# One hybrid layer (attention, S5, mixture of experts): another order for the work between the attention scores and the output projection

## The chip, the cores and the metric

The kernel runs on one core of a Trainium2 chip. The metric is the device time of one execution in microseconds (us), lower is better. Engines are named as in the profile: PE is TensorE, DVE is VectorE, ACT is ScalarE, POOL is GpSimd, SP is SyncE, whose queue issues nearly all loads here.

## What is computed

One layer on 272 token rows (16 learned meta tokens and 256 frames) of width 1024. The attention and an S5 state-space model run beside each other on projections of the same rows; their outputs are put side by side and multiplied with `w_out`. Then come a residual, a layer norm, and a mixture of 32 experts, four per token.

```python
h = layer_norm(concat(meta_tokens, x), ln_in_g, ln_in_b)
proj = h @ w_in                                  # q, k, v, u
# 4 heads, each the difference of two softmaxes
p = softmax(q @ k.T + bias)                      # masked by chunks of 64 frames
w = p[0] - lam * p[1]
att = rms_norm(w @ v, subln_g) * (1 - lam_init)
# S5: 32 groups of 16 channels, 64 states each
y = C @ scan(Abar, Bbar @ u) + d_skip * u
y = gelu(y); ssm = y * sigmoid(y @ w_glu + b_glu)
mix = concat(att, ssm) @ w_out
h = layer_norm(2 ** 0.25 * h + mix, ln1_g, ln1_b)
# router: top 4 of 32 experts, softmax over the four
ffn = sum over the four of gate * (((up + 1) * g * sigmoid(1.702 * g)) @ w_down + b_down)
out = layer_norm(2 ** 0.25 * h + ffn, ln2_g, ln2_b)[16:]
```

## The kernel before

The kernel is one function. It is written out by hand: each engine has one queue and works through it in the order in which the program issues its instructions, waiting at each for the semaphores of what it needs. An instruction that waits holds everything behind it on its engine. So the order of the calls in the program is the order of the work on every engine.

**The stages.** First the input rows are normalized (`hr`, kept for the residual) and projected to u, q, k and v. Beside the projections VectorE, GpSimd and ScalarE build the S5 matrices. Four frames make one step of the scan; inside such a step the output depends on the input through *lag blocks*, small matrices for lags 0 to 3. Then come the attention scores and the part that this change is about, the mix, the norm, the router, and a sorting of the tokens by expert. The longest stage is the last: the weights of the 32 experts, 384 chunks of 1 MiB, stream through a ring of 19 buffers (half-tiles) while TensorE multiplies. `load_to(n)` issues the chunk loads up to number n from SyncE, in order; a load waits until its buffer is free, and holds the loads behind it.

**From the scores to the mix**, in program order:

- *Lag blocks.* Matmuls write the products of all lags into one PSUM bank (`kb_`). VectorE builds the lag diagonal from a copied identity (`m32`) and the skip weights (`Dm`), eight pieces. `lag_b` (L719) copies the bank to SBUF (`KS`, ScalarE), adds the diagonal (VectorE), and copies 16 pieces into the padded lag matrix `ML`, eight on each of the two engines (L728, L730).
- *Value projections.* `values(h)` (L641) projects the values of head h and copies them out of PSUM (`vT`, L643). `value_rows(h, vT)` (L646) transposes them and copies them to `vr` with ScalarE (L650, L651). Heads 0 and 1 are done before; `values(2)`, `lag_b`, `values(3)` follow, then the load of the attention half of `w_out` (`wo0`), the router and bias loads, and `split_w(1, ...)`.
- *Rounding.* `split_w(j, ...)` (L568) prepares four 128-row tiles of `w_out`, j = 1 the S5 half and j = 0 the attention half. ScalarE rounds each (128 x 1024) to a high part (L572), VectorE subtracts it for the low part (L574). The mix adds three products: high by high, low weight by high row, high weight by low row (`cl`).
- *Attention products.* `av_a(i)` (L758 and on) does block i of 128 query rows: per head it transposes the weights, copies them to `wT` (ScalarE the full 128-row parts, L767; VectorE the 16-row part, L768), and multiplies with `vr` (L783), one head behind the transposes. Block 0 sees 144 keys, block 1 sees 272. In block 0 each head is followed by two pieces of `residual_rows` (L500): VectorE multiplies a 128 x 512 piece of `hr` by the norm's gain or adds its bias (L505), eight pieces in all. `av_b(i)` squares and sums the result (ScalarE, L791), takes the power -1/2 (GpSimd, L195) and scales (VectorE, L793). `av_c(i)` transposes it back (L800) and writes high and low parts (VectorE, L802 and L803).
- *S5 outputs.* `out_a(fb)` adds a lag product (L813) and two state products (L815) for four groups of 128 columns, evicted by ScalarE (`yt`, L818). `out_b` transposes two of them (L826) and does the GELU, ending in a tanh (L833); `out_c` writes `gy`.
- *Mix.* `mix(i, kbs)` (L863) accumulates the three products for tiles kbs of `w_out` and rows of block i, in four PSUM banks. The four attention tiles come first. Between them `split_bias` splits the experts' biases into three bf16 pieces (VectorE and ScalarE, L875 to L884). Then the gate: four matmul groups with `w_glu`, a sigmoid (ScalarE), a multiplication (VectorE, L900), and high and low parts (L901, L902). The S5 tiles of the mix follow (from 158.50 us on).

PSUM banks are given out in rotation by `nb()`: who takes a bank waits for the last reader of the one that had it eight banks before. The calls around the change stand in this order: `av_a(0)`, `av_b(0)`, half a rounding of `wo0`, `out_a(0)`, `out_a(1)`, `av_a(1)` with the other half inside, `av_c(0)`, `av_b(1)`, `out_b(0)`, `out_a(2)`, `out_a(3)`, `load_to(7)`, `out_c(0)`, `av_c(1)`, `out_b(1)`, then the mix.

Of the kernel before, what the change touches and what calls it, by code (L numbers as in the profile page):

```python
# [15 lines left out]
AF = mybir.ActivationFunctionType  # L16
OP = mybir.AluOpType
# [47 lines left out]
def hybrid_layer(ctx, tc, I, out):  # L65
    nc = tc.nc
    V, S, G, T, SP = nc.vector, nc.scalar, nc.gpsimd, nc.tensor, nc.sync
# [6 lines left out]
    PS = psp.tile([128, 8, 512], F32, name="PS")  # L74
# [9 lines left out]
    def slot(i, shape, name, dt=F32):  # L84
        return per.tile(shape, dt, name=name, tag=f"slot{i}")
# [414 lines left out]
    def residual_rows(n):  # L500

        for _ in range(n):
            i, h, j = rr_todo.pop(0)
            hf = hr[:, i, h * 512:(h + 1) * 512]
            V.tensor_tensor(hf, hf, bc[:, j, h * 512:(h + 1) * 512], op=(OP.mult, OP.add)[j])  # L505
# [54 lines left out]
    def load_to(n):  # L560
        while nload[0] < min(n, len(stream)):
            chunk(nload[0])
            nload[0] += 1
# [4 lines left out]
    def split_w(j, s_, l_, ks):  # L568
        if j not in W_HI:
            W_HI[j], W_LO[j] = parts4(s_, "wh", FR), parts4(l_, "wl", FR)  # L570
        for k in ks:
            S.activation(W_HI[j][k], W_OUT[j][k], AF.Copy)  # L572
        for k in ks:
            V.tensor_sub(W_LO[j][k], W_OUT[j][k], W_HI[j][k].bitcast(F32))  # L574
# [66 lines left out]
    def values(h):  # L641
        vT = lw([128, NP], "vT", bufs=2)
        S.activation(vT, proj("v", h, 0), AF.Copy)  # L643
        return vT

    def value_rows(h, vT):  # L646
        b = nb()
        for blk, n in ((0, 128), (1, 128), (2, 16)):
            T.transpose(PS[:n, b, blk * 128:blk * 128 + 128], vT[:, blk * 128:blk * 128 + n], ident)
        S.activation(vr[:, 0:2, h * 128:(h + 1) * 128], PS[:, b, 0:256].rearrange("p (a e) -> p a e", a=2), AF.Copy)  # L650
        S.activation(vr[:16, 2, h * 128:(h + 1) * 128], PS[:16, b, 256:384], AF.Copy)  # L651
# [45 lines left out]
    def lt_(shape, name, tag=None, bufs=None):  # L697
        return lpool.tile(shape, F32, name=name, tag=tag or name, bufs=bufs)

    kb_ = nb()  # L700
# [10 lines left out]
                         AB[:, ri, P, 0:3].rearrange("p t g c -> p (t g c)"), start=(ri == 0), stop=(ri == 1))  # L711
    Dm = lt_([128, 4, 32], "Dm", tag="y1")
    m32 = lt_([128, 32], "m32")
    for q in range(4):
        V.tensor_copy(m32[32 * q:32 * q + 32], ident[32 * q:32 * q + 32, 32 * q:32 * q + 32])
    for fb in range(4):
        V.tensor_scalar(Dm[:, fb], m32, DSK[:, fb:fb + 1], None, op0=OP.mult)

    def lag_b():  # L719
        KS = lt_([128, 4, 128], "KS", tag="y0")  # L720
        S.activation(KS, PS[:, kb_].rearrange("p (f c) -> p f c", f=4), AF.Copy)
        V.tensor_add(KS[:, :, 0:32], KS[:, :, 0:32], Dm)
        for j in range(4):
            for t in range(4):
                dst = ML[32 * t:32 * t + 32, :, j, 32 * t:128]
                srcv = KS[32 * j:32 * j + 32, :, 0:128 - 32 * t]
                if t < 2:
                    V.tensor_copy(dst, srcv)  # L728
                else:
                    S.activation(dst, srcv, AF.Copy)  # L730

    vt0 = values(2)
    lag_b()
    load_to(3)
    vt1 = values(3)
    wo0 = slot(3, [128, 4, D], "wo0")
    W_OUT[0] = [wo0[:, k] for k in range(4)]
    load(wo0, "w_out", 0, [[D, 128], [128 * D, 4], [1, D]])
# [5 lines left out]
    load(rk, "order_table", 0, [[2 * NE + 5, 128], [1, 2 * NE + 5]])  # L744
    for j, n in enumerate(("b_gate", "b_up", "b_down")):
        load(bf[32 * j:32 * j + 32], n, 0, [[D, 32], [1, D]])
    split_w(1, 5, 0, (0, 1, 2, 3))
    value_rows(2, vt0)
    value_rows(3, vt1)
    load_to(5)  # L750


    cat = mt([128, 8, NT], "cat", FR, tag="hTcat")
# [4 lines left out]
    def av_a(i, between=None):  # L758
        blks = ((0, 128), (1, 16)) if i == 0 else ((0, 128), (1, 128), (2, 16))
        nf = len(blks) - 1  # L760
        wts = []
        for h in range(4):
            tb = nb()
            for blk, n in blks:
                T.transpose(PS[:n, tb, blk * 128:blk * 128 + 128], PW[h, i][:, blk * 128:blk * 128 + n], ident)
            wT = lt_([128, 3, 128], "wT", bufs=2)
            S.activation(wT[:, :nf], PS[:, tb, :nf * 128].rearrange("p (a q) -> p a q", a=nf), AF.Copy)  # L767
            V.tensor_copy(wT[:16, nf], PS[:16, tb, nf * 128:nf * 128 + 128])  # L768
            wts.append(wT)
            if i == 0:  # L770
                residual_rows(2)
            if h == 1 and between:
                between()
            if h == 0:
                ob = nb()
            else:
                av_mm(i, h - 1, wts[h - 1], ob, blks, nf)
        av_mm(i, 3, wts[3], ob, blks, nf)
        OB[i] = ob
# [6 lines left out]
    def av_b(i):  # L786
        ob = OB[i]
        ss = lt_([128, 4], "ss")
        on = lt_([128, 4, 128], "on")
        for h in range(4):  # L790
            S.activation(on[:, h], PS[:, ob, h * 128:(h + 1) * 128], AF.Square, accum_out=ss[:, h:h + 1])  # L791
        rstd_of(ss, ss, EPS, 1.0 / 128)
        V.tensor_tensor(on, PS[:, ob].rearrange("p (h e) -> p h e", h=4), ss[:, :, None].to_broadcast([128, 4, 128]),  # L793
                        op=OP.mult)
        ON[i] = on

    def av_c(i):
        b = nb()
        for h in range(4):
            T.transpose(PS[:, b, h * 128:(h + 1) * 128], ON[i][:, h], ident)  # L800
        srcv, c_ = PS[:, b].rearrange("p (h e) -> p h e", h=4), slice(i * 128, (i + 1) * 128)
        V.tensor_scalar(cat[:, 0:4, c_], srcv, subg, None, op0=OP.mult)  # L802
        V.scalar_tensor_tensor(cl[0][:, :, c_], srcv, subg, cat[:, 0:4, c_].bitcast(F32), op0=OP.mult, op1=OP.subtract)  # L803
# [18 lines left out]
    def out_b(f2):  # L822
        b = nb()
        for f in range(2):
            for t in range(4):
                T.transpose(PS[:, b, f * 256 + t * 64:f * 256 + t * 64 + 64],  # L826
                            YT[2 * f2 + f][:, t * 128:(t + 1) * 128], ident[:64, :64])
        hy, ya = (lt_([128, 2, 4, 64], f"y{j}") for j in range(2))
        S.activation(hy, PS[:, b].rearrange("p (f t c) -> p f t c", f=2, t=4), AF.Copy)
        S.activation(ya, hy, AF.Square)  # L830
        V.tensor_scalar(ya, ya, 4 * 0.044715, 1.0, op0=OP.mult, op1=OP.add)
        V.tensor_mul(ya, ya, hy)
        S.activation(ya, ya, AF.Tanh, scale=2.0 * math.sqrt(2.0 / math.pi))  # L833
        HY[f2] = hy, ya
# [5 lines left out]
                                   op0=OP.add, op1=OP.mult)  # L840

    av_a(0)
    av_b(0)
    split_w(0, 8, 2, (0, 1))
    out_a(0)
    out_a(1)
    av_a(1, lambda: split_w(0, 8, 2, (2, 3)))
    av_c(0)
    av_b(1)
    out_b(0)  # L850
    out_a(2)
    out_a(3)
    load_to(7)
    out_c(0)
    av_c(1)
    out_b(1)


# [28 lines left out]
    out_c(1)  # L887
    split_bias()
    mix(1, range(2))
    mix(0, range(2, 4))  # L890
    mix(1, range(2, 4))
    gs = lw([128, 4, NT], "gs", tag="aw1")
# [658 lines left out]
```

## Time and profile before

| | |
|---|---|
| time, median of 3 runs | 1141.91 us (1139.74 to 1143.63) |
| the profiled execution | 1141.39 us, of which the profile's span is 1139.6 us |
| mean granted TensorE clock | 0.954 |
| TensorE matmul busy | 1021.1 us (90%) |
| VectorE busy | 365.6 us (32%) |
| ScalarE busy | 159.7 us (14%) |
| GpSimd busy | 106.5 us (9%) |
| loads of the main queue | 424.58 MB, 91.5% of the 16 DMA engines' time |

A busy share is an average over the whole span. Most of the span is the expert stage; the stretch of the change lies between about 100 and 172 us. The timelines of the engines in that stretch give, for each run of instructions of one line, its start, its length and their count, and in brackets how long the engine had been idle and what it had waited for. A float32 matmul appears as two records. The granted clock is the share of 2.4 GHz that TensorE was given.

### The profile page before, as it was taken

How to read it: one execution, taken by the hardware profiler on the slowest of the kernel's cores; microseconds unless marked ns; L12 is line 12 of the kernel's file. 1: busy time of each engine (PE TensorE's matmuls, PEld its weight loads, DVE VectorE, ACT ScalarE, POOL GpSimd, SP SyncE). 2: the span in 40 equal slices, each digit the busy share in tenths (PEclk: the TensorE clock that was granted, in tenths of full speed). 3: DMA queues.
4: the chain of work that ended last, by engine and by line, in shares of the span. 5: the costliest groups of instructions: out<-in, count | busy, mean ns of one | idle time of the engine just before them, and what ended most of it. 6: DMA issues, size and time to landing. Idle time of an engine off the chain costs nothing. (4 is left out here: it accounts for less than half of the span.)

```text
span 1139.6 us, 16409 instructions
## 1 busy us (share of the span) xinstructions
PE 1021.1 (90%) x6572; PEld 523.6 (46%) x6572; DVE 365.6 (32%) x755; ACT 159.7 (14%) x329; POOL 106.5 (9%) x223
## 2 busy tenths in 40 slices
PE   6986997899999788998999977799999999998665
PEld 5875884344554244444444423354453444453222
DVE  7999664223122212321131221122223212232103
ACT  1735423000010000111001000010001000001000
POOL 2300004101100110021001010101101010010001
PEclk9989898999999999998999987999999999999698
DMA  7725286999999999999999999999999999999795
GB/s 220 282 95 173 96 343 263 379 371 420 420 421 422 420 420 421 421 421 419 422 422 420 420 421 421 421 420 421 421 422 421 421 421 401 422 420 420 309 419 229
DMA packets 72313, 425.67 MB, mean 374 GB/s; under 512 B 14925, under 2 KB 15546, under 8 KB 23210
## 3 DMA queue, kind: packets, MB, share of 16 engines
q1 hardware_dynamic: 72234, 424.58, 91.5%
q8 instruction: 53, 0.87, 0.3%
q14 instruction: 26, 0.21, 0.1%
HBM read 423.50 MB, written 1.87 MB: 373 GB/s over the span
## 5 line engine op out<-in xcount | busy, mean ns | idle before, releaser
L1206 PE MATMUL PS<-wx,xgp 128*32 128x256 f32 (+2 forms) x3008 | 485.4, 493 | 30.6 <-DMA wx<-in_w_gate 20.9
L1206 PEld LDWEIGHTS PS<-wx,xgp 128*32 128x32 f32 (+2 forms) x3008 | 184.9, 133 | 292.9 <-issue 204.8
L1206 PE MATMUL PS<-wx,yT 128*32 128x256 f32 (+2 forms) x1504 | 230.3, 467 | 18.2 <-DMA wx<-in_w_down 16.2
L1206 PEld LDWEIGHTS PS<-wx,yT 128*32 128x32 f32 (+2 forms) x1504 | 90.7, 127 | 141.6 <-issue 89.8
L948 POOL COPY si<-P 96x32 bf16<-96x32 bf16 (+2 forms) x32 | 7.4, 233 | 755.4 <-PE PS L1200 725.5
L1253 DVE COPY yc<-PS 32x256 f32<-32x256 f32 (+1 forms) x39 | 20.0, 514 | 164.1 <-ACT yc L1255 164.1
L1159 PEld LDWEIGHTS PS<-ohp,hr 128*128 128x128 f32 x512 | 63.5, 200 | 8.4 <-issue 8.4
L1159 PE MATMUL PS<-ohp,hr 128*128 128x128 f32 x512 | 65.8, 288 | 0.2 <-DVE ohp L1151 0.2
L1228 DVE TENSOR_SCALAR PS<-PS 128x256 f32<-128x256 f32 (+2 forms) x33 | 22.6, 683 | 115.5 <-PE PS L1206 115.5
L1200 PE MATMUL PS<-B,si 96*32 96x256 bf16 (+2 forms) x282 | 40.2, 336 | 16.5 <-SPq L1309 9.6
L1222 DVE TENSOR_SCALAR g<-PS 128x256 f32<-128x256 f32 (+1 forms) x27 | 14.9, 553 | 120.5 <-PE PS L1206 120.4
L1239 DVE COPY yT<-PS 128x512 f32<-128x512 f32 (+1 forms) x39 | 22.7, 594 | 88.2 <-PE PS L1238 88.2
L1255 ACT ACTIVATE yc<-PS 32x256 f32<-32x256 f32 (+1 forms) x39 | 17.4, 446 | 231.2 <-PE PS L1206 224.9
L1290 DVE SCALAR_TENSOR_TENSOR lo<-yc,gc,hi 128x1024 fp32r<-128x1024 f32 x15 | 19.3, 1284 | 86.8 <-ACT hi L1289 85.5
L1304 DVE TENSOR_TENSOR acc<-PS,acc 128x1024 f32<-128x1024 f32 x30 | 35.4, 1220 | 14.7 <-PE PS L1301 14.6
L1163 ACT ACTIVATE xgp<-PS 128x512 f32<-128x512 f32 x16 | 9.6, 598 | 210.3 <-PE PS L1159 210.3
L1200 PEld LDWEIGHTS <-si 96*32 96x32 bf16 (+2 forms) x282 | 11.4, 101 | 49.2 <-issue 46.6
L1223 ACT ACTIVATE PS<-g 128x256 f32<-128x256 f32 (+1 forms) x27 | 13.2, 491 | 144.4 <-DVE g L1222 144.4
L1149 POOL TENSOR_SCALAR gop<-io,PMs,Gs 128x32 f32<-128x32 f32 (+2 forms) x60 | 33.2, 568 | 0.0
L1222 DVE TENSOR_SCALAR yc<-PS 128x1024 f32<-128x1024 f32 x6 | 7.3, 1225 | 78.5 <-PE PS L1206 78.5
L1301 PE MATMUL PS<-hi,gt 128*128 128x512 f32 x60 | 26.2, 437 | 3.0 <-ACTq L1309 3.0
L1247 ACT ACTIVATE yc<-PS 128x1024 f32<-128x1024 f32 x6 | 6.1, 1025 | 138.0 <-PE PS L1206 138.0
(389 smaller groups left out, 865.1 us busy)
## 6 DMA issues: line engine op xcount, KB each, us to landing
wx<-in_w_gate SPq DMA_DIRECT2D x128, 1024.0 KB, 19.7
wx<-in_w_up SPq DMA_DIRECT2D x128, 1024.0 KB, 19.8
wx<-in_w_down SPq DMA_DIRECT2D x127, 1024.0 KB, 19.7
w_u<-in_w_in SPq DMA_DIRECT2D x2, 1024.0 KB
w_q<-in_w_in SPq DMA_DIRECT2D x1, 2048.0 KB
w_k<-in_w_in SPq DMA_DIRECT2D x2, 1024.0 KB
w_v<-in_w_in SPq DMA_DIRECT2D x1, 2048.0 KB
wo<-in_w_out SPq DMA_DIRECT2D x2, 1024.0 KB
```

Source lines behind the costliest of these rows:

```text
L1149: eng.tensor_scalar(dst[:, i, o:o + m], iv, pc, gg[:, i, t:t + 1], op0=OP.is_equal, op1=OP.mult)
L1159: T.matmul(PS[:, 4 + h, k * 128:k * 128 + n], hr[:, i, rows_of(db)], oh_[:, i, :n], start=(i == 0), stop=(i == 1))
L1200: T.matmul(o, sel[:, :m], B96[:, w, f * n:f * n + n], start=True, stop=False)
L1206: T.matmul(PS[(f % nf) * m:(f % nf) * m + m, b + f // nf, :n], xT(kb), c[:, f * n:f * n + n], start=False, stop=(kb == 7))
L1222: V.tensor_scalar(g_, r_, 7.0, None, op0=OP.min)
L1228: V.tensor_scalar(r_, r_, 7.0, -7.0, op0=OP.min, op1=OP.max)
L1239: V.tensor_copy(yT[:, 4 * a:4 * a + nk], PS[:, b, :nk * 128].rearrange("p (k s) -> p k s", k=nk))
L1253: V.tensor_copy(d_, s_)
L1255: S.activation(d_, s_, AF.Copy)
L1290: V.scalar_tensor_tensor(lo[:n], YC[g][:n], GC[g][:n], hi[:n].bitcast(F32), op0=OP.mult, op1=OP.subtract)
L1301: T.matmul(PS[:, 4 + 2 * i + h], GT[g][:n, i * 128:(i + 1) * 128], part[:n, h * 512:(h + 1) * 512], start=(j == 0), stop=(j == 1))
L1304: V.tensor_tensor(acc[:, i].rearrange("p (h c) -> p h c", h=2), PS[:, 4 + 2 * i:6 + 2 * i], acc[:, i].rearrange("p (h c) -> p h c", h=2), ...
```

## The change

It puts the same work into another order, and moves eight small operations to another engine:

- The lag diagonal (`m32`, `Dm`) is built by GpSimd in place of VectorE.
- The lag products leave their PSUM bank right behind the value projection of head 2. The rest of `lag_b`, the add and the sixteen copies, comes behind the first attention product (`av_a(0)`).
- The value rows of heads 2 and 3 follow their projections at once, ahead of the load of `wo0`.
- The rounding of the S5 half of `w_out`, which stood ahead of the value rows, is cut in two, on both sides of the second attention product. The rounding of the attention half is cut in two as well: behind `av_b(1)`, and behind `av_c(1)`.
- The second attention product comes ahead of the first two S5 outputs, `av_b(1)` behind them.
- The chunk loads 2 and 3 (`load_to(3)`) and 4 and 5 (`load_to(5)`) are issued later.
- The eight residual pieces leave the first attention product and stand behind the first attention tiles of the mix.

```diff
-        V.tensor_copy(m32[32 * q:32 * q + 32], ident[32 * q:32 * q + 32, 32 * q:32 * q + 32])
+        G.tensor_copy(m32[32 * q:32 * q + 32], ident[32 * q:32 * q + 32, 32 * q:32 * q + 32])
     for fb in range(4):
-        V.tensor_scalar(Dm[:, fb], m32, DSK[:, fb:fb + 1], None, op0=OP.mult)
+        G.tensor_scalar(Dm[:, fb], m32, DSK[:, fb:fb + 1], None, op0=OP.mult)
 
     def lag_b():
-        KS = lt_([128, 4, 128], "KS", tag="y0")
-        S.activation(KS, PS[:, kb_].rearrange("p (f c) -> p f c", f=4), AF.Copy)
         V.tensor_add(KS[:, :, 0:32], KS[:, :, 0:32], Dm)
...
     vt0 = values(2)
-    lag_b()
-    load_to(3)
+    S.activation(KS, PS[:, kb_].rearrange("p (f c) -> p f c", f=4), AF.Copy)
     vt1 = values(3)
+    value_rows(2, vt0)
+    value_rows(3, vt1)
     wo0 = slot(3, [128, 4, D], "wo0")
...
-    split_w(1, 5, 0, (0, 1, 2, 3))
-    value_rows(2, vt0)
-    value_rows(3, vt1)
-    load_to(5)
...
             wts.append(wT)
-            if i == 0:
-                residual_rows(2)
             if h == 1 and between:
...
     av_a(0)
+    load_to(3)
+    lag_b()
     av_b(0)
-    split_w(0, 8, 2, (0, 1))
+    split_w(1, 5, 0, (0, 1))
+    av_a(1)
+    split_w(1, 5, 0, (2, 3))
+    av_c(0)
     out_a(0)
     out_a(1)
-    av_a(1, lambda: split_w(0, 8, 2, (2, 3)))
-    av_c(0)
     av_b(1)
+    load_to(5)
+    split_w(0, 8, 2, (0, 1))
     out_b(0)
     out_a(2)
     out_a(3)
     load_to(7)
     out_c(0)
     av_c(1)
+    split_w(0, 8, 2, (2, 3))
     out_b(1)
...
     mix(1, range(2))
+    residual_rows(8)
     mix(0, range(2, 4))
```

Line numbers of the changed kernel are one lower in `lag_b`, four to six lower from `av_a` to `out_c`, and one higher from the gate on. The names with numbers are tiles: `wo_794` and `wo_795` are the halves of the S5 half of `w_out`, `wo_983` (before) and `wo_973` (changed) the attention half; `MG` holds the lag matrix.

ScalarE, from the value copy of head 3 to the first half of the attention half's rounding; before, the lag copies (L730) stand ahead of the first row here:

```order
L643 ACTIVATE vT<-PS 128x272
L572 ACTIVATE wh<-wo_794 128x1024 x2
L572 ACTIVATE wh<-wo_795 128x1024 x2
L650 ACTIVATE vr<-PS 128x2x128
...
L767 ACTIVATE wT<-PS 128x128 x4
L791 ACTIVATE on,ss<-PS 128x128 x4
L572 ACTIVATE wh<-wo_983 128x1024 x2
L818 ACTIVATE yt<-PS 64x4x4x32 x2
L767 ACTIVATE wT<-PS 128x256 x2
```

The same stretch of the changed kernel, from the first product's operand on:

```order
L763 ACTIVATE wT<-PS 128x128 x4
L729 ACTIVATE MG<-KS 32x4x64
L729 ACTIVATE MG<-KS 32x4x32
...
L785 ACTIVATE on,ss<-PS 128x128 x4
L572 ACTIVATE wh<-wo_794 128x1024 x2
L763 ACTIVATE wT<-PS 128x256 x4
L572 ACTIVATE wh<-wo_795 128x1024 x2
L812 ACTIVATE yt<-PS 64x4x4x32 x2
L785 ACTIVATE on,ss<-PS 128x128 x4
L572 ACTIVATE wh<-wo_973 128x1024 x2
```

Between the operands of the first product (four copies of 128x128) and those of the second (128x256) stood the squares, two roundings and two evictions; now there stand eight lag copies, the squares and two roundings.

TensorE in the changed kernel, at the transposes of the first two S5 outputs and the third lag product, with the waits that the instructions carry (`AB` and `X` are the state products' operands):

```order
L820 MATMUL PS<-ident,yt 128x64 [waits Activation_49]
L820 MATMUL PS<-ident,yt 128x64 x3
L820 MATMUL PS<-ident,yt 128x64 [waits Activation_49]
L820 MATMUL PS<-ident,yt 128x64 x3
L807 MATMUL PS<-MG,u_433 64x128 [waits DVE_49,Activation_49]
L809 MATMUL PS<-AB,X 64x128 x2
```

The third lag product (L807) waits for VectorE and ScalarE here: its PSUM bank is that of the second attention product, which ScalarE squares and VectorE scales. Before, its bank was that of the second S5 output, and the instruction had no wait.

VectorE in the changed kernel, from the second attention product's high and low parts to the first gate multiplication (`bf`, `bp`, `bq` are the biases and their pieces):

```order
L796 TENSOR_SCALAR cat<-PS,subg 128x4x128
L797 SCALAR_TENSOR_TENSOR cl<-PS,subg,cat 128x4x128
L574 TENSOR_TENSOR wl<-wo_973,wh 128x1024 x2
L825 TENSOR_SCALAR y_1213<-y_1213 128x512
L826 TENSOR_TENSOR y_1213<-y_1213,y_1212 128x512
L833 SCALAR_TENSOR_TENSOR gy<-y_1213,y_1212 128x4x64 x2
L879 TENSOR_TENSOR bf<-bf,bp 96x1024
L881 TENSOR_TENSOR bq<-bf,bq 96x1024
L884 COPY B_1219<-bp 32x1024 x3
L884 COPY B_1219<-bq 32x1024 x6
L505 TENSOR_TENSOR hr<-hr,bc 128x512 x8
L901 TENSOR_TENSOR gs<-gs,gy 128x256
```

Two rows are new at this place: the two subtractions (L574) ahead of the GELU of the last S5 outputs, and the eight residual pieces (L505) ahead of the gate multiplication (L901). All other rows stood there in the same order.

## Rows read from the trace of the kernel before

**Rows 1.** The page's part 2: DMA share in tenths, GB/s, 40 slices of 28.5 us.

```profile
DMA  7725286999999999999999999999999999999795
GB/s 220 282 95 173 96 343 263 379 371 420 420 421 422 420 420 421 421 421 419 422 422 420 420 421 421 421 420 421 421 422 421 421 421 401 422 420 420 309 419 229
```

**Rows 2.** Windows: stretch, length, busy by PE, PEld, DVE, ACT, POOL; PEclk; DMA share; GB/s.

```profile
184.00:194.00 10.00, 9.21 (x42) 5.32 (x41) 6.82 (x30) 0.00 (x0) 2.77 (x1) 0.66 0.07 11
```

**Rows 3.** Timeline of TensorE: start, length, line, operation, output, inputs, count [idle before].

```profile
104.46 0.49 PE L649 MATMUL PS<-ident,vT 128*128 128x128 f32 x3
107.71 0.55 PE L649 MATMUL PS<-ident,vT 128*128 128x128 f32 x3 [2.76 <-ACT vT L643]
...
112.63 0.80 PE L783 MATMUL PS<-vr,wT 128*128 128x128 f32 x2 [3.93 <-ACT wT L767]
...
116.61 2.80 PE L783 MATMUL PS<-vr,wT 128*128 128x128 f32 x8
...
127.35 1.12 PE L783 MATMUL PS<-vr,wT 128*128 128x128 f32 x6
...
133.95 0.43 PE L813 MATMUL PS<-MG,u 128*64 128x128 f32 x2
...
139.34 0.66 PE L800 MATMUL PS<-ident,on 128*128 128x128 f32 x4
...
140.56 0.50 PE L868 MATMUL PS<-wh,cat 128*128 128x512 f32 x1
...
161.24 0.39 PE L870 MATMUL PS<-wh,cl 128*128 128x512 f32 x1
```

**Rows 4.** Windows of 1 us: the granted clock is the third number from the end.

```profile
109.00:110.00 1.00, 0.00 (x0) 0.00 (x0) 1.00 (x2) 1.00 (x2) 0.00 (x0) 0.50 1.02 410
122.00:123.00 1.00, 1.00 (x8) 1.00 (x7) 1.00 (x2) 0.49 (x1) 0.00 (x0) 0.67 0.00 0
```

**Rows 5.** Timeline of ScalarE.

```profile
104.28 2.96 ACT L730 ACTIVATE MG<-KS 32x256 f32<-32x256 f32 x8 [1.98 <-issue]
...
107.68 3.90 ACT L572 ACTIVATE wh<-wo 128x1024 fp32r<-128x1024 f32 x4
...
119.45 0.28 ACT L791 ACTIVATE on<-PS 128x128 f32<-128x128 f32 x1 [2.32 <-PE PS L783]
...
120.47 2.02 ACT L572 ACTIVATE wh<-wo 128x1024 fp32r<-128x1024 f32 x2
...
126.44 0.59 ACT L818 ACTIVATE yt<-PS 64x512 f32<-64x512 f32 x1 [2.03 <-PE PS L815]
...
143.21 0.63 ACT L833 ACTIVATE y<-y 128x512 f32<-128x512 f32 x1 [1.22 <-DVE y L832]
```

**Rows 6.** Timeline of VectorE.

```profile
113.52 1.39 DVE L505 TENSOR_TENSOR hr<-hr,bc 128x512 f32<-128x512 f32 x2
...
121.95 0.69 DVE L793 TENSOR_TENSOR on<-PS,ss 128x512 f32<-128x512 f32 x1 [1.15 <-POOL ss L195]
...
128.66 2.36 DVE L574 TENSOR_TENSOR wl<-wo,wh 128x1024 fp32r<-128x1024 f32 x2 [0.67 <-ACT wh L572]
...
155.54 0.42 DVE L900 TENSOR_TENSOR gs<-gs,gy 128x256 f32<-128x256 f32 x1 [3.38 <-ACT gs L899]
...
160.31 0.43 DVE L902 TENSOR_TENSOR cl<-gs,cat 128x256 fp32r<-128x256 f32 x1 [0.49 <-ACT cat L901]
...
173.39 1.21 DVE L963 SCALAR_TENSOR_TENSOR n<-m,r 128x1 f32<-128x1 f32 x1 [0.67 <-POOL r L195]
...
1130.88 0.16 DVE L1482 SCALAR_TENSOR_TENSOR f<-f,f 128x1 f32<-128x1 f32 x1
```

**Rows 7.** Timeline of GpSimd.

```profile
120.88 1.03 POOL L195 TENSOR_TENSOR ss<-ss,mhalf 128x4 f32<-128x4 f32 x1 [67.27 <-DVE ss L194]
...
173.32 1.26 POOL L979 TENSOR_TENSOR hr<-hr,bc 128x512 f32<-128x512 f32 x1
```

**Rows 8.** GpSimd's groups of one shape: count, busy us, mean ns, idle before.

```profile
L1151 POOL TENSOR_SCALAR ohp<-io,PMs 128x32 f32<-128x32 f32 x28 | 9.5, 359 | 0.0
```

More of the change, by code (lines that the diff above doesn't have):

```diff
@@ L713, in hybrid_layer @@
     m32 = lt_([128, 32], "m32")
+    KS = lt_([128, 4, 128], "KS", tag="y0")
     for q in range(4):
-        V.tensor_copy(m32[32 * q:32 * q + 32], ident[32 * q:32 * q + 32, 32 * q:32 * q + 32])
+        G.tensor_copy(m32[32 * q:32 * q + 32], ident[32 * q:32 * q + 32, 32 * q:32 * q + 32])
     for fb in range(4):
-        V.tensor_scalar(Dm[:, fb], m32, DSK[:, fb:fb + 1], None, op0=OP.mult)
+        G.tensor_scalar(Dm[:, fb], m32, DSK[:, fb:fb + 1], None, op0=OP.mult)
     def lag_b():
-        KS = lt_([128, 4, 128], "KS", tag="y0")
-        S.activation(KS, PS[:, kb_].rearrange("p (f c) -> p f c", f=4), AF.Copy)
         V.tensor_add(KS[:, :, 0:32], KS[:, :, 0:32], Dm)
```

## The prediction

> **What bounds the kernel now.** I read the page first. Its line of DMA shares by slice [rows 1] shows two parts: six slices (some 170 us) of projections, attention and S5 with gaps, then the stream of expert weights at 9 tenths nearly to the end. The stream can only run ahead as far as its 19 half-tiles; after that each load waits for a buffer that TensorE has used up. So I read the windows next: between 184 and 194 us, just before the first expert matmuls, the DMA engines are 7% busy [rows 2]. The ring is full and waits for TensorE. **Whatever moves TensorE's start on the experts moves the end by as much**, as long as the loads that the change delays still fit into that hole. So the question is only when TensorE gets through the stretch from 104 to 172 us.
>
> TensorE's timeline there [rows 3]: the value projections end at 104.5; the second value transposes wait 2.76 us for ScalarE; the first attention product waits 3.93 us for ScalarE; the mix (the output projection) starts at 140.56. Between, the granted clock falls: 0.50 in the microsecond after 109, 0.67 in that after 122 [rows 4], so 1.2 GHz from 109 to 122.7. Before the fall the engine had done 0.9 us of transposes between two waits; before the rise it had run lag products without a gap since 119.4. The waits at 105 to 112 are what the change goes at.
>
> **The change, step by step.** All times are of the profiled execution (1141.39 us, 0.52 below the median of the runs shown), in its own clock.
>
> *The first product comes early.* The value copy no longer stands behind eight lag-block copies on ScalarE (2.96 us), nor the value rows behind four roundings (3.90 us) [rows 5]. The copy follows the projection at 104.6, the transposes end at 105.6, and the first product runs at full clock: a matmul is 1.12/3 = 0.37 us [rows 3], eight of them and their transposes take 4.4 us. On VectorE its small copies are no longer followed by 1.39 us of residual rows each [rows 6]. It ends at 109.9 instead of 119.4: 9.5 us gained.
>
> *A new wait takes its place.* What stood ahead of the first product on ScalarE now stands between the products, as the order shows. The lag add waits on VectorE for the first product's last small copy (109.5); then ScalarE does the lag copies (2.96), the squares (1.0, from 119.45 to 120.47) and two roundings (half of 3.90) [rows 5], so the second product's first operand leaves at 115.8. TensorE has only two heads' transposes for that time, to 110.7: it waits 5.1 us. VectorE's part of the operand comes behind a power on GpSimd (1.03 [rows 7]), the scaling (0.69) and two subtractions (2.36 [rows 6]): 118.1, another 1.0 us of waiting.
>
> *The clock.* 5.1 us with nothing is more than the 3.93 beside which it fell before, so I take the rest of the second product at 1.2 GHz: 0.70 a matmul (2.80 for four [rows 3]), as all of the first product ran before. It ends at 126.4; at full clock at 122.2. These are the two ends.
>
> *The lag products.* Transposes (0.6) and eight groups follow; eight took 139.34 - 133.95 = 5.4 us [rows 3], 5.3 without the hand-over. They end at 132.2, and with the eviction (0.59 [rows 5]) and 0.7 of transposes TensorE is at 133.5 where it was at 133.95 before: **the 9.5 us are gone.** Next, the third lag product now takes the PSUM bank of the second attention product (eight banks on in the rotation; before, it was that of a lag product long evicted). It waits for that product's squares, which stand on ScalarE behind both evictions, and for its power and scaling: 0.6 + 1.0 + 0.2 + 1.03 + 0.69 and hand-overs from 132.4, so 136.1, a wait of 2.7 us. From there to the mix it is 140.56 - 133.95 = 6.6 us [rows 3] as before: 142.6. A second fall there, or a rise as late as before (3.3 us into the lag products), costs 1.9 more: 144.5. With 1.2 GHz through both the first lag products and the third, 147.8. I take 144.5, since two waits of over 2.5 us stand within 25 us: **+3.9 us.**
>
> *The residual rows.* Eight pieces, 4 x 1.39 = 5.5 us [rows 6], leave the first product, where they lay beside half-clock matmuls, and go onto VectorE between the bias pieces and the gate multiplications. VectorE is idle there for 3.38 us [rows 6]. But the bias pieces come later as well: the second columns' scaling and two subtractions (2.36) now stand ahead of the last tanh, which moves from 2.65 us behind the mix's start [rows 3, 5] to 4.6. So the bias pieces end 13.6 instead of 11.6 us behind it, the rows 19.1, and the first gate multiplication starts there instead of at 15.0 (155.54 [rows 6]): 4.1 us late. TensorE needs the result: the last low part was ready at 160.74, the matmul that reads it started at 161.24 [rows 3, 6]. So 0.5 of it is covered, and nothing else is. **+3.6 us**; the lower end, if the tanh kept its place, is 5.5 - 3.4 - 0.5 = 1.6.
>
> *Without cost.* The lag diagonal on GpSimd: eight pieces at 0.36 by the nearest row [rows 8], 2.9 us; GpSimd was idle for the 67.27 us up to 120.88 [rows 7], and they wait for old loads and ScalarE alone; if that cover went, the lag add at 109.1 would wait. VectorE's saving there lies behind the first product's copies and shortens nothing. SyncE: the second and third chunk go behind the first half of W_out, which waits for TensorE's value projections in any case; they are first read at 190. The fourth chunk waits for the last subtraction, which ended at 131.0 [rows 6], some 148 now. From there sixteen chunks (2.5 us each at 420 GB/s, the rate of most slices in rows 1) and 1 MB of norm weights take 42 us: 190, against 202 for the ring's next free buffer. The hole of rows 2 covers it; without it the loads would be the bound.
>
> **Sum**: 3.9 + 3.6 = +7.5 us on 1141.39: **1148.9 us**. The chain behind (norm, router, first gather) starts from TensorE's mix and hides nothing.
>
> **A rule against the change.** A VectorE operation of one column with two SBUF inputs took 1.21 us at 173.39, beside a GpSimd piece of 1.26 that began 0.07 earlier, and 0.16 when GpSimd was done [rows 6, 7]. So GpSimd pieces can hold VectorE. The Trainium skill (SBUF — State Buffer, section "SBUF: two separate sides") says that the two engines share a port pair as an exclusive lock, and that a VectorE operation with two SBUF inputs is blocked while a GpSimd operation that reads SBUF holds it; by that rule the 1.21 is a wait, and the trace agrees. From the rows: if the diagonal's pieces ran beside the scores' chain on VectorE, which gates TensorE, they would add up to 2.9 us; if at 53.6, when GpSimd falls idle (120.88 - 67.27), and VectorE copies out of PSUM, nothing. I take nothing.
>
> **Rivals.**
> - *The clock holds* in the 5.1 us gap: the mix starts at 138.8, so -1.8, with +3.6 behind it: +1.8, 1143.2. Against it: it fell beside a shorter wait. It decides at a granted clock of 1.00 from 110 to 130. Chance 0.13.
> - *The rows are hidden* (faster). If the residual pairs had been what set the pace from 112.6 to 119.4, their 5.5 us would come back whole, with the lag work on ScalarE under cover: 1135.9. It needs 5.5 us of VectorE's idle time ahead of the gate multiplications; the trace has 3.38. Chance 0.05.
> - *GpSimd holds VectorE* during the scores: 7.5 + 2.9, 1151.8. For it the 1.21 us row, against it what the pieces wait for. Chance 0.07.
> - *Forecast*: chance 0.75, from 1145.0 (mix at 142.6, rows 1.6) to 1153.1 (mix at 147.8, rows 4.5, where the gate's waits bring the low clock too).
>
> **The numbers.** A measurement of this kernel tells some 0.3% from no change: 3.4 us, so 1138.5 to 1145.3 about the median. The forecast and the held VectorE lie above but for the last 0.3 of its lower end (0.82), the holding clock within (0.13), the hidden rows below (0.05). The range runs from the holding clock, 1143.2, to the forecast's upper end, 1153.1; the hidden rows and a tenth for tails stay out.
>
> **What would show it.** Right: TensorE idle some 5 us behind the second product's first transposes, released by ScalarE; a granted clock of 0.50 behind it; the third lag product released by VectorE's scaling; no idle time on VectorE ahead of the gate multiplications, and TensorE waiting some 2 us for them at the mix's second half; the DMA engines still idle before the first expert. Wrong: no wait behind those transposes, the mix before 140, or a gate multiplication less than 15.5 us behind the mix's start.

## The result and the profile after

The changed kernel takes 1151.37 us (median of 6 runs, 1149.88 to 1154.16), the kernel before 1142.13 us (6 runs, 1139.74 to 1144.32): a ratio of 1.0084 with a 95% interval from 1.0071 to 1.0096. That is 9.2 us slower, inside the range that was forecast, and 2.5 us above the number.

The profiled execution of the changed kernel took 1152.58 us, 1.2 above its median, with a span of 1150.8 us, 11.2 more than the span before. First, where along the way these 11.2 us arise. Three rows of TensorE's timeline of the kernel before that the prediction did not need (start, length, line, operation, count):

```profile
15.59 14.91 PE L408 MATMUL PS<-hT,w_u 128*128 128x272 f32 x64 [1.60 <-DVE e L254]
...
169.10 1.03 PE L974 MATMUL PS<-ident,hr 128*128 128x128 f32 x8
...
189.84 4.17 PE L1206 MATMUL PS<-wx,xgp 128*64 128x512 f32 x16
```

They are the projection to u at the start, the first transposes behind the norm, and the first matmuls of the experts. The same engine in the changed kernel:

```profile
15.61 16.97 PE L408 MATMUL PS<-hT,w_u 128*128 128x272 f32 x64 [1.40 <-DVE e L254]
...
105.86 0.49 PE L649 MATMUL PS<-ident,vT 128*128 128x128 f32 x3
106.57 0.55 PE L649 MATMUL PS<-ident,vT 128*128 128x128 f32 x3 [0.22 <-ACT vT L643]
...
107.89 0.90 PE L777 MATMUL PS<-vr,wT 128*128 128x128 f32 x4 [0.34 <-ACT wT L763]
...
117.47 1.22 PE L777 MATMUL PS<-vr,wT 128*128 128x128 f32 x4 [5.03 <-ACT wT L763]
119.82 0.79 PE L777 MATMUL PS<-vr,wT 16*128 16x128 f32 x2 [1.13 <-DVE wT L764]
...
128.27 0.69 PE L807 MATMUL PS<-MG,u 128*64 128x128 f32 x2
...
139.61 0.66 PE L807 MATMUL PS<-MG,u 128*64 128x128 f32 x2 [2.73 <-DVE on L787]
...
146.45 0.66 PE L794 MATMUL PS<-ident,on 128*128 128x128 f32 x4
...
147.68 0.50 PE L868 MATMUL PS<-wh,cat 128*128 128x512 f32 x1
...
179.53 1.03 PE L975 MATMUL PS<-ident,hr 128*128 128x128 f32 x8
...
200.74 3.65 PE L1207 MATMUL PS<-wx,xgp 128*64 128x512 f32 x16
```

Against [rows 3] and the rows above, with each start in both kernels:

| point | before | changed | later by | of it new here |
|---|---|---|---|---|
| value projections end (transposes start) | 104.46 | 105.86 | 1.40 | 1.40 |
| mix starts | 140.56 | 147.68 | 7.12 | 5.72 |
| norm done for the first rows | 169.10 | 179.53 | 10.43 | 3.31 |
| first expert matmul | 189.84 | 200.74 | 10.90 | 0.47 |
| span | 1139.6 | 1150.8 | 11.2 | 0.3 |

The first 1.4 us are not the change's. Up to there both kernels issue the same work, apart from the lag diagonal, which comes later than the cause: the u projection took 16.97 us in this execution and 14.91 in the one of before. In the profiles of the eight runs below the transposes started between 105.1 and 106.7 us in seven, among them the one whose program is that of before up to this point (the second run, 105.1), and at 104.1 in the eighth. So the execution of before that the prediction started from was an early one. The 0.5 us behind the norm need not be the change's either: that stretch took between 20.4 and 21.6 us in the ten profiles, with the same work in all. What is left for the change is 5.7 + 3.3 = 9.0 us, beside 9.2 in the medians.

The waits that the prediction named are in the rows: 5.03 us for ScalarE ahead of the second attention product, 1.13 for VectorE inside it, and 2.73 for VectorE's scaling at the third lag product. The old ones (2.76 and 3.93 us [rows 3]) have become 0.22 and 0.34. ScalarE's timeline of the changed kernel shows what the 5.03 us consist of:

```profile
111.03 2.96 ACT L729 ACTIVATE MG<-KS 32x256 f32<-32x256 f32 x8 [0.54 <-DVE KS L721]
113.99 0.28 ACT L785 ACTIVATE on<-PS 128x128 f32<-128x128 f32 x1
...
115.14 2.00 ACT L572 ACTIVATE wh<-wo 128x1024 fp32r<-128x1024 f32 x2
117.03 0.66 ACT L763 ACTIVATE wT<-PS 128x256 f32<-128x256 f32 x2
```

Lag copies, squares, roundings, one behind the other without a gap, and only then the operand. The windows show the clock (third number from the end) and, in the last row, the DMA engines:

```profile
112.00:114.00 2.00, 0.44 (x5) 0.15 (x2) 1.93 (x6) 1.93 (x7) 0.00 (x0) 1.00 1.03 291
...
118.00:120.00 2.00, 0.87 (x5) 0.57 (x4) 1.96 (x4) 0.00 (x0) 0.00 (x0) 0.50 1.01 422
130.00:132.00 2.00, 2.00 (x12) 2.00 (x11) 0.00 (x0) 0.00 (x0) 0.00 (x0) 0.50 0.00 0
...
140.00:142.00 2.00, 2.00 (x12) 2.00 (x11) 2.00 (x3) 0.41 (x1) 0.00 (x0) 0.50 0.00 0
...
196.00:200.00 4.00, 3.87 (x18) 3.57 (x18) 3.23 (x11) 0.00 (x0) 2.37 (x1) 0.50 0.02 6
```

TensorE ran at 1.2 GHz from about 115.4 to 132.4 us and again from about 139.2 to 142.7. The last row stands just ahead of the first expert matmul: 2% DMA share, the ring is full and waits for TensorE, as before [rows 2]. The later loads cost nothing: they ran on to about 195 us, where the forecast had 190, and the first expert matmul did not wait for them.

On VectorE, ahead of the gate:

```profile
158.42 2.58 DVE L884 COPY B<-bq 32x1024 bf16<-32x1024 bf16 x6
161.03 5.40 DVE L505 TENSOR_TENSOR hr<-hr,bc 128x512 f32<-128x512 f32 x8
166.35 0.42 DVE L901 TENSOR_TENSOR gs<-gs,gy 128x256 f32<-128x256 f32 x1
```

There is no idle time left where 3.38 us were [rows 6]: bias pieces, residual rows, gate multiplication. TensorE waits for it at the mix's second half, by the view of waits (total, times, longest):

```profile
PE PS L868 <- ACT cat L902: 2.2, 4, 1.3
```

### The profile page after: what moved, and what is told of

It reads as the page before. It is cut to its first block, busy times and chain, and to the rows that moved or that the text cites. A ratio compares the mean times of both kernels' runs of the same rounds, so it can differ in the third digit from the quotient of the medians.

```text
span 1150.8 us, 16405 instructions
## 1 busy us (share of the span) xinstructions
PE 1026.7 (89%) x6572; PEld 528.1 (46%) x6572; DVE 364.7 (32%) x747; ACT 159.5 (14%) x329; POOL 108.9 (9%) x231
## 5 line engine op out<-in xcount | busy, mean ns | idle before, releaser
L1207 PE MATMUL PS<-wx,yT 128*32 128x256 f32 (+2 forms) x1504 | 230.3, 467 | 17.3 <-DMA wx<-in_w_down 15.2
L1302 PE MATMUL PS<-lo,gt 128*128 128x512 f32 x60 | 24.6, 410 | 0.8 <-DVE lo L1291 0.8
```

The costliest lines, as they stand in the source:

```text
L1207: T.matmul(PS[(f % nf) * m:(f % nf) * m + m, b + f // nf, :n], xT(kb), c[:, f * n:f * n + n], start=False, stop=(kb == 7))
L1302: T.matmul(PS[:, 4 + 2 * i + h], GT[g][:n, i * 128:(i + 1) * 128], part[:n, h * 512:(h + 1) * 512], start=(j == 0), stop=(j == 1))
```

## The experiments

Eight kernels, each timed beside the kernel before on its chip. Times are medians; the ratio is to the kernel before. Starts of single instructions are compared from the end of the value projections on, or from the mix's start on, so that a slow or fast beginning drops out.

### The residual rows in another gap

```diff
+    residual_rows(8)
     av_b(1)
...
     mix(1, range(2))
-    residual_rows(8)
```

> The changed kernel with one thing undone: the eight residual pieces leave the place behind the mix's first half and stand in VectorE's idle 7.5 us ahead of the second attention product's squares (129.9 to 137.4 in the changed kernel's trace). Theory (the rows hold the gate multiplications): the first gate multiplication comes 15.2 us behind the mix's start instead of 18.7, TensorE no longer waits 2.2 us at the mix's second half, and the whole is 3.3 us faster than the changed kernel: 1148.1, still 6 above the kernel before. Rival (the rows only took the place of a wait that was there anyway, the bias pieces or the table load before the sigmoid): no change, 1151.4.

Measured: 1147.31 us, ratio 1.0047 (1.0030 to 1.0063), 4.1 below the changed kernel. VectorE and TensorE:

```profile
129.42 5.39 DVE L505 TENSOR_TENSOR hr<-hr,bc 128x512 f32<-128x512 f32 x8
...
162.28 0.42 DVE L901 TENSOR_TENSOR gs<-gs,gy 128x256 f32<-128x256 f32 x1 [1.90 <-ACT gs L900]
```

```profile
147.06 0.50 PE L869 MATMUL PS<-wh,cat 128*128 128x512 f32 x1
...
164.99 0.59 PE L869 MATMUL PS<-wh,cat 128*128 128x512 f32 x1
```

The first gate multiplication starts 15.2 us behind the mix's start (18.7 in the changed kernel) and waits for ScalarE, not for VectorE's own queue; the mix's second half starts without a wait, 17.93 us behind the mix's start, as in the kernel before (158.50 - 140.56 = 17.94). From the mix's start to the norm it is 28.5 us as before, and 31.9 in the changed kernel. The rows cost about what stood in the sum, at that place, and the rival (they replace another wait) is out.

### The residual rows alone

```diff
             wts.append(wT)
-            if i == 0:
-                residual_rows(2)
...
     mix(1, range(2))
+    residual_rows(8)
```

This is the kernel before with that one edit.

> The kernel before with the residual rows alone moved behind the mix's first half. Theory: 5.4 us of rows meet 3.4 us of idle time on VectorE and 0.5 us of slack at the mix, so 1.5 us slower than before: 1143.6; the first attention product stays as slow as it was, since it ran at 1.2 GHz beside the rows. Rival 1 (the rows set the pace of the first product): 5.5 us faster, 1136.6. Rival 2 (the rows find no cover at all, as if the bias pieces were as late as in the changed kernel): 5 us slower, 1147.

Measured: 1144.03 us, ratio 1.0014 (1.0005 to 1.0024), 1.7 above before. VectorE at the gate, and TensorE in the first product and at the mix:

```profile
153.33 5.40 DVE L505 TENSOR_TENSOR hr<-hr,bc 128x512 f32<-128x512 f32 x8
158.65 0.42 DVE L899 TENSOR_TENSOR gs<-gs,gy 128x256 f32<-128x256 f32 x1
```

```profile
117.28 2.80 PE L781 MATMUL PS<-vr,wT 128*128 128x128 f32 x8
...
141.71 0.50 PE L866 MATMUL PS<-wh,cat 128*128 128x512 f32 x1
```

The first product without rows is as slow as with them: its last matmuls take 2.80 us in both [rows 3]. So the rows were hidden there, and the rival in which they had set the pace (faster by 5.5) is out. At the gate the multiplication comes 16.94 us behind the mix's start instead of 14.98: 2.0 late, of which the mix's slack takes a part, and the norm comes 30.1 us behind it instead of 28.5: 1.6. The other 1.7 us of the changed kernel's 3.3 come from the bias pieces, which it has made late.

### The PSUM bank of the third lag product

```diff
     out_b(0)
+    nb()
     out_a(2)
```

> The changed kernel with one PSUM bank skipped in the rotation ahead of the third S5 output, so that it no longer takes the bank of the second attention product. Theory (that bank is the cause of the 2.73 us wait and of the second fall of the clock): the third lag product follows the transposes with no wait, the granted clock stays at 1.00 from 134 us to the mix, and the mix starts some 2.4 us earlier (4.1 us earlier for the lag products, of which ScalarE takes some back, since the third output's eviction then waits for the tanh ahead of it): 1149.0. Rival (the wait stood in front of another one for the same scaling): the wait moves to the second attention product's transposes and the mix starts within 0.5 us of where it was: 1151.

Measured: 1147.77 us, ratio 1.0043 (1.0026 to 1.0060), 3.6 below the changed kernel. The third lag product follows without a wait. TensorE at the mix, and two windows:

```profile
143.98 0.94 PE L820 MATMUL PS<-ident,yt 64*128 64x64 f32 x8 [1.14 <-ACT yt L812]
144.85 0.50 PE L869 MATMUL PS<-wh,cat 128*128 128x512 f32 x1
```

```profile
140.00:144.00 4.00, 2.86 (x26) 2.45 (x24) 3.27 (x6) 1.58 (x4) 0.00 (x0) 1.00 0.02 4
...
146.00:148.00 2.00, 2.00 (x7) 1.50 (x6) 2.00 (x2) 1.42 (x3) 0.00 (x0) 0.51 0.01 4
```

The mix starts 2.8 us earlier (38.97 us behind the end of the value projections, 41.82 in the changed kernel), near the 2.4 that ScalarE's evictions were to leave. The bank is the cause of the wait. One part of the theory fell: the second fall of the clock did not go, it came later, into the mix, where the first 1.2 GHz matmuls of 0.63 us follow transposes and a wait of 1.14 us. The gate's matmuls start 12.78 us behind the mix's start instead of 11.21; since TensorE had waited 2.2 us for the residual rows there and now waits 0.9, the end does not show it.

### The second product right behind the first

```diff
     av_a(0)
     load_to(3)
-    lag_b()
-    av_b(0)
-    split_w(1, 5, 0, (0, 1))
-    av_a(1)
-    split_w(1, 5, 0, (2, 3))
+    av_a(1, lambda: av_b(0))
+    lag_b()
+    split_w(1, 5, 0, (0, 1))
+    split_w(1, 5, 0, (2, 3))
```

> The changed kernel with the second attention product right behind the first: its operands leave ScalarE ahead of the lag copies and of both roundings, and the first product's squares and scaling are issued inside it, behind its second head. Theory (what stands on ScalarE between the two products makes the 5 us wait and the fall of the clock): no wait over 2 us between the products, the second one at 2.4 GHz and ended by 119 instead of 127; the lag copies then make a shorter wait ahead of the lag products, and the mix starts 5 to 7 us earlier: 1145.5. Rival (ScalarE's total of work before the lag products is what counts, in any order): the wait of 5 us and the fall of the clock move whole to the lag products, and the mix starts at most 2 us earlier: 1149.5 or more.

Measured: 1141.90 us, ratio 1.0006 (0.9993 to 1.0018), 9.5 below the changed kernel and at the time of before. TensorE, two windows and a wait at the mix's second half:

```profile
115.43 0.52 PE L761 MATMUL PS<-ident,aw 128*128 128x128 f32 x3 [1.04 <-DVE on L787]
...
129.31 0.66 PE L807 MATMUL PS<-MG,u 128*64 128x128 f32 x2 [2.76 <-DVE on L787]
...
138.54 0.50 PE L867 MATMUL PS<-wh,cat 128*128 128x512 f32 x1
```

```profile
118.00:120.00 2.00, 2.00 (x9) 1.67 (x10) 1.90 (x6) 1.92 (x6) 0.00 (x0) 0.50 1.02 422
...
128.00:134.00 6.00, 4.69 (x22) 4.72 (x23) 4.79 (x7) 2.68 (x4) 0.44 (x1) 0.50 0.00 0
```

```profile
PE PS L867 <- ACT cat L901: 2.2, 4, 1.3
```

The longest wait between the products is 1.04 us, the second product is done at 117.9, and the mix starts 33.3 us behind the value projections' end instead of 41.8: 8.5 us, more than the 5 to 7 expected. The rival (the same work on ScalarE only waits elsewhere) is out: the lag products start at 118.91 with no wait, since each needs only its own quarter of the lag copies; the shorter wait that the theory had there did not come either. This does not make the 5 us wait the cause of the whole loss. The residual rows still cost 3.3 us (the norm comes 31.9 us behind the mix's start, as in the changed kernel); they are paid for by a mix that starts 2.8 us earlier than in the kernel before (33.3 us against 36.1). The clock still falls twice, for about 3.5 us at the first lag products and from 128 to about 134.7 behind the bank's 2.76 us.

### The roundings behind the second product

```diff
-    split_w(1, 5, 0, (0, 1))
     av_a(1)
+    split_w(1, 5, 0, (0, 1))
     split_w(1, 5, 0, (2, 3))
```

> The changed kernel with the first two roundings of the S5 half moved behind the second attention product, so that between the two products ScalarE has the lag copies and the squares alone. Theory (the wait is the sum of what stands on ScalarE between the products): the wait of 5.0 us at the second product becomes 3.0, VectorE's 1.1 us wait behind it goes, the clock still falls but later or for a shorter time, and the mix starts 2 to 4 us earlier: 1148.5. Rival (the lag copies and the first product's scaling alone hold the second product for as long, the roundings lie beside them): 1151.

Measured: 1148.64 us, ratio 1.0061 (1.0040 to 1.0082), 2.7 below the changed kernel. TensorE:

```profile
112.80 1.54 PE L761 MATMUL PS<-ident,aw 128*128 128x128 f32 x6
116.44 1.22 PE L777 MATMUL PS<-vr,wT 128*128 128x128 f32 x4 [2.10 <-ACT wT L763]
118.41 0.79 PE L777 MATMUL PS<-vr,wT 16*128 16x128 f32 x2 [0.75 <-DVE wT L764]
```

```profile
112.00:114.00 2.00, 2.00 (x9) 1.47 (x8) 1.93 (x6) 1.94 (x6) 0.00 (x0) 0.50 1.03 381
```

The waits of 5.03 and 1.13 us are 2.10 and 0.75 (3.0 and none expected), and the mix starts 2.1 us earlier against the value projections. ScalarE begins the operand 4.1 us behind the start of its lag copies instead of 6.0, and the two roundings take 2.0: so the wait is a sum over what stands on ScalarE. The first wait shrinks by 2.9 us and not by 2.0 because TensorE comes to it later: its clock had fallen at 111.9 us already, and the product and the six transposes ahead of the wait (1.54 us, 0.88 in the changed kernel) ran partly or wholly at 1.2 GHz. The theory had the clock fall later or for a shorter time; it fell earlier, ahead of the wait, which began at 114.3.

### The lag diagonal back on VectorE

```diff
-        G.tensor_copy(m32[32 * q:32 * q + 32], ident[32 * q:32 * q + 32, 32 * q:32 * q + 32])
+        V.tensor_copy(m32[32 * q:32 * q + 32], ident[32 * q:32 * q + 32, 32 * q:32 * q + 32])
...
-        G.tensor_scalar(Dm[:, fb], m32, DSK[:, fb:fb + 1], None, op0=OP.mult)
+        V.tensor_scalar(Dm[:, fb], m32, DSK[:, fb:fb + 1], None, op0=OP.mult)
```

> The changed kernel with the lag diagonal back on VectorE. Theory (it costs nothing on either engine, since GpSimd does it at 53 us beside copies, and VectorE would do it behind the first product's chain of scores, where its next work waits for ScalarE): within 0.3% of the changed kernel, 1151.4 (1149 to 1153). Rival (GpSimd's pieces hold VectorE): up to 2.9 us faster, 1148.5. Rival 2 (the eight pieces on VectorE stand ahead of the first product's small copies): up to 1.4 us slower, 1152.8.

Measured: 1151.74 us, ratio 1.0093 (1.0070 to 1.0116): the changed kernel's ratio lies inside. VectorE does the eight pieces while it would have waited for ScalarE's operand:

```profile
103.00 0.72 DVE L716 COPY m<-ident 32x32 f32<-32x32 f32 x4
103.76 0.68 DVE L718 TENSOR_SCALAR Dm<-m,VC 128x32 f32<-128x32 f32 x4
```

The engine of the diagonal makes no difference that these runs can show.

### All three remedies in one

The kernel with the second product first, with the skipped bank, four residual pieces between the first product's copies on VectorE and four ahead of `out_c(0)`:

```diff
             wts.append(wT)
+            if i == 0 and h:
+                residual_rows(2 if h == 3 else 1)
...
     out_b(0)
+    nb()
     out_a(2)
     out_a(3)
     load_to(7)
+    residual_rows(4)
     out_c(0)
...
     mix(1, range(2))
-    residual_rows(8)
```

> The kernel with the second product first (x4), and besides the skipped PSUM bank (x3) and the residual rows out of the mix: four pieces between the first product's small copies on VectorE, four ahead of the gating of the first S5 outputs. Theory (the two costs that x4 keeps, the 2.76 us wait for the bank and the 2.2 us wait at the gate, are independent of each other and of the order of the products): 2.8 less at the mix's start and 3.3 less behind it, so 1141.9 - 6 = 1136, 0.5% faster than the kernel before. Rival (as in the run with the free bank alone, ScalarE and a later fall of the clock take back what the bank gives): 1139.

Measured: 1137.46 us (12 runs), ratio 0.9966 (0.9953 to 0.9978): 0.3% faster than before, between theory (1136) and rival (1139). TensorE at the mix:

```profile
134.69 0.71 PE L871 MATMUL PS<-wh,cat 128*128 128x512 f32 x1
```

The mix starts 4.0 us earlier than with the second product first alone, but the clock falls into it again, from 134.8 to 138.2 us, and its first half takes 12.77 us instead of 11.22. The costs do not add up freely: the fall of the clock moves to the next place.

### An order that gives TensorE something between the waits

```diff
+    residual_rows(1)
+    V.tensor_add(KS[:, :, 0:32], KS[:, :, 0:32], Dm)
+    lag_b((0, 1))
+    split_w(1, 5, 0, (1,))
+    lag_b((2, 3))
+    value_rows(2, vt0)
...
+    av_h(0, 0)
+    split_w(1, 5, 0, (0,))
+    residual_rows(1)
+    split_w(1, 5, 0, (3,))
+    out_a(1)
+    value_rows(3, vt1)
...
+    out_a(0)
+    av_h(0, 1)
...
+    av_b(0)
+    out_b(0)
...
+    av_h(1, 0)
+    residual_rows(1)
+    out_a(2)
+    av_c(0, nb())
+    split_w(0, 8, 2, (0,))
+    out_a(3)
+    av_h(1, 1)
...
     mix(0, range(2))
+    av_c(1, c1b)
+    mix(0, range(2, 4))
```

`av_h(i, h)` is one head of an attention product. The lag copies come first, and all four S5 outputs stand between the heads. The diff shows a part of the added lines only.

> An order of its own, with the same work: the lag copies ahead of the attention products, and the S5 outputs (lag and state products) set between the attention products and between their heads, so that TensorE has something to do while ScalarE copies, rounds and squares; roundings one tile at a time; residual rows singly where VectorE waits; the second attention output's transposes and the bias pieces inside the mix. All roundings of the S5 half still come ahead of those of the attention half. Theory (what costs time in this stretch is TensorE standing between two waits, not the amount of work on any engine): mix's start some 9 us earlier than in the kernel before (131 to 133 us), no gap over 2 us, the whole 8 to 10 us faster than before: 1133. Rival 1 (the expert stream is not ready so early, since the loads wait for the roundings and the ring fills by 190 us): TensorE waits for weights at the first expert, 1139 or more. Rival 2 (ScalarE's 20 us of work in the stretch is the bound in any order): as the combined kernel, 1136.

Measured: 1129.89 us, ratio 0.9902 (0.9884 to 0.9920): 1% faster than before, and 21 us below the changed kernel. TensorE and two windows:

```profile
127.50 0.51 PE L894 MATMUL PS<-wh,cat 128*128 128x512 f32 x1
...
157.18 1.03 PE L1001 MATMUL PS<-ident,hr 128*128 128x128 f32 x8
```

```profile
104.00:132.00 28.00, 28.00 (x204) 23.34 (x203) 23.20 (x41) 19.23 (x51) 2.06 (x2) 1.00 0.52 172
...
180.00:190.00 10.00, 9.26 (x54) 4.28 (x52) 1.39 (x5) 1.03 (x2) 0.00 (x0) 1.00 0.78 262
```

From 104 to 132 us TensorE is busy all the time, at full clock, with ScalarE busy 19.2 and VectorE 23.2 of the 28 us. The mix starts 13.1 us earlier than in the kernel before, the norm is done 11.9 earlier, and the end comes 11.4 earlier. Neither rival holds: the experts' first matmuls, at 178.62, do not wait for weights, and ScalarE's work fits beside TensorE's. The run changes the whole order at once, so it does not tell how much each move gives, nor how much of the gain is the clock's.

## Why the prediction was right

**What bounds the kernel.** Right: the first expert matmul came 10.9 us later, the span grew by 11.2, and the DMA engines stood idle ahead of it. In all ten kernels, with that start between 178.6 and 200.7 us, the end came 948 to 950 us behind it.

**The first product comes early.** Right: the two waits at 105 to 112 us are down to 0.22 and 0.34, and the product ends at 111.6, which is 110.2 without the late beginning (109.9 predicted).

**A new wait takes its place.** Right in place, releaser and size: 5.03 us (5.1) and 1.13 (1.0). With the roundings moved the mix starts 2.1 us earlier; with the second product first the wait is gone and the mix starts 8.5 us earlier.

**The clock** is where the size was off. The forecast gave the second product 1.2 GHz, and so it was. Its reason, the length of the wait, is not shown. Without the wait (the second product first) the clock held up to 117.7 us, nearly to the product's end. But in two runs whose programs are the changed kernel's up to the wait (the residual rows in another gap, the roundings behind) it had fallen at 111.2 and 111.9 us, 1.4 and 2.5 us before the wait began; in the changed kernel it fell 2.9 us into it. So what made it fall there stays open, and how far the term was right by luck. For what follows it said that a second fall, or a rise as late as before, costs 1.9 more, and counted one of the two. Both came. The first eight lag groups took 135.67 - 128.27 = 7.4 us (5.3 at full clock), since the clock rose only at 132.4; the last eight took 146.45 - 139.61 = 6.8, since it fell again near the end of the 2.73 us wait. That is 3.6 us, 1.7 over the 1.9 of the sum: the attention stretch came to 5.7 us instead of 3.9. In the prediction's clock, without the late beginning, the mix started at 146.3, between the 144.5 of the sum and the upper end that it named (147.8, with 1.2 GHz through both).

**The PSUM bank.** Right: 2.73 us (2.7), released by VectorE's scaling, and gone when one bank is skipped.

**The residual rows.** Right: 3.3 us (3.6), shown by moving them away (3.3 in the trace, 4.1 in the medians) and by moving them alone (1.7, with 1.6 as the lower end). The multiplication started 18.7 us behind the mix's start where 19.1 stood.

**Without cost.** Right for the lag diagonal, by its own run, and for the loads. The rival in which GpSimd's pieces hold VectorE is out. Three rows of the changed kernel show the two engines side by side, first GpSimd, then VectorE:

```profile
53.53 0.95 POOL L716 COPY m<-ident 32x32 f32<-32x32 f32 x4
```

```profile
53.45 0.23 DVE L335 TENSOR_TENSOR eb<-pw,xs 128x64 f32<-128x64 f32 x1
53.60 0.23 DVE L336 TENSOR_TENSOR eb<-xs,pw 128x64 f32<-128x64 f32 x1
```

VectorE was not yet copying out of PSUM here; the forecast had assumed that it was. L335 began ahead of the first GpSimd copy; L336, also with two SBUF inputs, began 0.07 us behind that copy's start, and both took 0.23 us. The row of 1.21 us in the kernel before stood beside a GpSimd piece of 1.26 [rows 6, 7]; the copies here take some 0.2 us each. The Trainium skill (SBUF — State Buffer, section "SBUF: two separate sides") has such an operation blocked while GpSimd holds the shared ports; with pieces this short the row shows no such wait.

**The sum**: 3.9 + 3.6 = 7.5 predicted; 5.7 + 3.3 = 9.0 in the trace, 9.2 in the medians. Of the 2.5 us by which the time lies above the number, 1.7 are the change's, by size the second cost of the clock, and 0.7 come from the start: the sum began from an execution of 1141.39 us, and the median of the kernel before is 1142.13.

**The rivals.** The clock did not hold (1.00 up to about 115 only), the rows were not hidden, and GpSimd's pieces cost nothing that shows in the time.

## What to carry to other kernels

Where engines work through queues in a fixed order, taking one product early gains nothing by itself: read off what now stands ahead of the next operand on the engine that copies it, and who takes which PSUM bank eight allocations later. TensorE's waits cost time here, and in nine of the ten kernels the clock fell somewhere in this stretch as well, though not always behind the longest. The three remedies together, which take the longest waits away, gained 3.8 us on the kernel before (1137.46 us); the order that puts independent matmuls between them had 28 us without a gap at full clock and gained 11.4. Work that is free beside one stage is not free in the next: ask for idle time on its engine at the new place, in the changed order.

## What had not been expected

Taking the bank's wait away did not keep the clock up. It fell later, in the mix, in two kernels (at about 146 and at 134.8 us), after waits of 0.29 and 1.14 (0.29 and 1.18) us only and the two groups of transposes ahead of the mix; the 1.2 GHz matmuls there took 0.63 us instead of 0.39, and the first half of the mix 1.6 us more. What in these small groups lets the clock fall was not separated.

The same 64 matmuls of the u projection took 14.91 us in one profiled execution and 16.97 in another, at a granted clock of 1.00 in both. They run beside the first loads; why they differ was not tried. A comparison of two single profiles can hold 1 to 2 us of that.
